# A gMLP / Mamba-2 / SwiGLU layer on one core: gating matmuls in halves, inverse roots one iteration later, running sums fetched earlier, and some stores issued by ScalarE

## The chip, the cores and the metric

The kernel runs as one program on one core of a Trainium2 chip. A core has five instruction streams that run by themselves and meet at semaphores: TensorE (PE in the profile; PEld is its weight load), VectorE (DVE), ScalarE (ACT), GpSimd (POOL) and SyncE (SP). SP computes nothing here; it issues the transfers between HBM and the on-chip memory, and before the change it issues every one of them. An engine works through its instructions in order, so an instruction that waits holds up all behind it on the same engine, a transfer that waits on SP included. The metric is device microseconds (us) from launch to end; a run's number is that of the core.

## The reference, cut to what matters

One layer on 2048 latent tokens of width 1024, with 256 context tokens that only feed the scan's first states:

```python
hl = _rms(x) * norm1_w * (1 + sc1) + sh1               # adaLN
proj = hl @ w_in                                       # u, v | z, x, B, C, dt
# group A: gated MLP, 8 heads of 128, chunks of 128 tokens
u, v = split(gelu(proj[..., :2048]), 2)
v = _rms(v per head) * gm_norm_w
mixed = einsum('hts,bcshd->bcthd', gm_ws, v) + gm_bs
gm_out = u * mixed
# group B: Mamba-2 scan forward and backward, 16 heads of 64, chunks of 128 tokens
xbc = silu(centred_conv(x, B, C))
y = ssd_forward(xbc, dt_f) + flip(ssd_backward(flip(xbc), flip(dt_b))) + xs * D
ssd_out = _rms(y * silu(z), per half of 512) * ssd_norm_w
x = x + g1 * (concat(gm_out, ssd_out) @ w_out)
x = x + g2 * swiglu(_rms(x) * norm2_w * (1 + sc2) + sh2)
out = _rms(x) * final_norm_w
```

In the scan a chunk's decay between two tokens is exp of a difference of running sums (`a_cs`) along the chunk.

## The kernel before

Every large product is in float32, split into a high and a low part: `mm3` (L224) runs three 128x512 matmuls for each of 8 pieces of the inner dimension, 24 for one output tile of 128x512, into one of three PSUM banks called `mmp`. Five more banks, `smp`, serve all else. Tokens are worked in two blocks of 1024. On-chip buffers of 128x520 floats come from a pool of 14, `tma`, which loads, temporaries and results waiting for their store all share. Results that later stages need go through HBM: `rec` (the convolved x, B, C by chunk), `fscr` (running sums), `zscr`, `mscr` (mixing), `gmscr`, `sscr` (scan output), `r3scr` (its inverse roots), `x2scr` (residual).

The stages in order: adaLN and the context (to about 100 us of the profiled span); `xbc` of block 1 (to about 281); **run 1**, with `proj_v`, `proj_u`, `proj_z` of block 1 as main work and the context states, the backward scan of chunks 15 to 8, input statistics and adaLN weights beside it (to 573); `xbc` of block 0 (to 765); **run 2** (765 to 1560); then the SwiGLU layer.

In run 2 the main work is `proj_z`, `proj_v`, `proj_u` of block 0 and four times `out_half` (the output product), 16 or 17 steps each, 113 in all; a step is one `mm3` with what follows it. Beside it `ssd_bwd` and `ssd_y` run as a generator that is advanced 2.61 steps for each step of main work (`SIDE`), which sets the order in which instructions are put on every engine.

`ssd_y` has 32 iterations, one for each chunk `c` and half `g`. In iteration i it loads the records of i+2, runs `y_seg` of i+1 (the decay matrices, in two quarters `q`: two running-sum rows spread over 128 partitions come in, ScalarE adds a bias at L757, VectorE subtracts and takes the minimum at L758, ScalarE exponentiates, GpSimd multiplies at L762), then `y_out` of i (TensorE products, sums, the product with `zscr` at L798, the square sums at L799), then `y_store` of i-1 (four transposes L806, a copy L808, a store L809). `y_seg` begins with the load of the backward state at L745. After every eighth iteration `y_rstd` works out the inverse roots of 512 tokens: 12 small VectorE instructions (L815 and `newton`, L242 to L247), a transpose on TensorE (L819), a copy (L821) and a store (L822).

`proj_v` collects four chunks `c` of `v`, normalises them, and then, while the next four are computed, runs `mixing` on them after the `mm3` of c = 2: for each of 4 heads it loads the head's 128x128 weights and its bias row (L627, L628) into one of two buffers `gw`, runs 4 matmuls (L631) and one VectorE instruction (L633). The last four chunks are mixed at the end, after the last step.

A store passed to `behind` is issued by `flush` (L584) after the next `mm3`.

Of the kernel before, what the change touches and what calls it, by code (L numbers as in the profile page):

```python
# [14 lines left out]
P = 128  # L15
# [6 lines left out]
TB = 512  # L22
# [61 lines left out]
def kernel(ctx: ExitStack, tc: tile.TileContext, xT, ctxp, cc, crow, wad1, wad2, vecs, rows,  # L84
# [244 lines left out]
    for k in range(KT):  # L329
        t = xin()  # L330
# [132 lines left out]
    def to_tok(o, n, q, ch):  # L463
        g, coff = (ch // 4, R_X + (ch % 4) * P) if ch < 8 else (ch - 8, R_B)
        nt = n // P
        ps = smp()
        for c in range(nt):
            PE.transpose(out=ps[:, c * P:(c + 1) * P], in_=o[:, c * P:(c + 1) * P], identity=ident)
        t = tma()
        S.copy(t[:, :n], ps[:, :n])  # L470
        DMA.dma_start(rec[q][g][:, :, coff:coff + P].rearrange("c p x -> p c x"),
                      t[:, :n].rearrange("p (c x) -> p c x", x=P))

    def xbc(blk, hs, hc, tail):
# [120 lines left out]
    def stat_terms(hs, c, us, off):  # L595
# [6 lines left out]
            r.append((hs[j][k][:, 0, cs], hs[j][k][:, 1, cs], hi[:, fs], lo[:, fs]))  # L602
        return r

    def proj_u(blk, hs):
        for h0 in range(0, 8, 2):
            us = [unit(U_U + h0), unit(U_U + h0 + 1)]
            for j in range(2):
                ts_ = slice((blk * 2 + j) * TB, (blk * 2 + j + 1) * TB)
                for i, (hi, lo) in enumerate(us):  # L610
                    m = tmp()
                    DMA.dma_start(m[:, :TB], mscr[h0 + i][:, ts_])
                    ps = mmp()
                    mm3(ps, [(hi[:, k * P:(k + 1) * P], lo[:, k * P:(k + 1) * P], hs[j][k][:, 0, :], hs[j][k][:, 1, :]) for k in range(KT)])
                    flush()
                    t = gelu2(ps, tmp)
                    V.tensor_tensor(out=t[:, :TB], in0=t[:, :TB], in1=m[:, :TB], op=ALU.mult)
                    behind(gmscr[h0 + i][:, ts_], t[:, :TB])
                    yield

    def proj_v(blk, hs):
        def mixing(hh, j, vh):
            ts_ = slice((blk * 2 + j) * TB, (blk * 2 + j + 1) * TB)
            for h in range(4):
                hd = hh * 4 + h
                gw = sp.tile([P, 2, P], F32, name="gw", tag="gw", bufs=2)
                DMA.dma_start(gw[:, 0, :], gmw[:, hd * P:(hd + 1) * P])  # L627
                DMA.dma_start(gw[:, 1, :], gmb[:, hd * P:(hd + 1) * P].broadcast_to([P, P]))  # L628
                ps = smp()
                for c in range(4):  # L630
                    PE.matmul(ps[:, c * P:(c + 1) * P], lhsT=vh[c][:, h * P:(h + 1) * P], rhs=gw[:, 0, :], start=True, stop=True)  # L631
                m = tmp()
                V.scalar_tensor_tensor(out=m[:, :TB].rearrange("p (c x) -> p c x", x=P), in0=ps.rearrange("p (c x) -> p c x", x=P),  # L633
                                       scalar=vec[:, V_GN + hd:V_GN + hd + 1], in1=gw[:, 1:2, :].broadcast_to([P, 4, P]),
                                       op0=ALU.mult, op1=ALU.add)
                behind(mscr[hd][:, ts_], m[:, :TB])

        prev = None
        for hh in range(2):
            us = [unit(U_V + hh * 4 + i) for i in range(4)]  # L640
            for j in range(2):
                vh = []
                ms = sml()[:, :16]
                for c in range(4):
                    ps = mmp()
                    mm3(ps, stat_terms(hs, j * 4 + c, us, 0))
                    flush()
                    v = gelu2(ps, xin)
                    sq = tmp()
                    for h in range(4):  # L650
                        S.activation(sq[:, h * P:(h + 1) * P], v[:, h * P:(h + 1) * P], AF.Square, accum_out=ms[:, c * 4 + h:c * 4 + h + 1])
                    vh.append(v)
                    if c == 2 and prev is not None:
                        mixing(*prev)
                    if c < 3:
                        yield
                V.tensor_scalar(out=ms, in0=ms, scalar1=1.0 / P, scalar2=4 * EPS, op0=ALU.mult, op1=ALU.add)
                r = newton(ms, 16)
                for c, v in enumerate(vh):
                    V.tensor_tensor(out=v[:, :TB].rearrange("p (a b) -> p a b", b=P), in0=v[:, :TB].rearrange("p (a b) -> p a b", b=P),  # L660
                                    in1=bc(r[:, c * 4:c * 4 + 4].rearrange("p (a o) -> p a o", o=1), P), op=ALU.mult)
                yield
                prev = (hh, j, vh)
        mixing(*prev)
        yield

    zdone = [0]
# [67 lines left out]

    hbp = []

    def y_load(pools, i, c, g):
        return {"rc": load_rec(pools[i % 3 == 2], c, g, True)}

    def y_seg(st, c, g):
        rc = st["rc"]
        Gt = []
        hb = hbp[0].tile([P, TB], F32, name="hb", tag="hb") if g else tma()[:, :TB]
        DMA.dma_start(hb, hscr[c][:, g * TB:(g + 1) * TB])  # L745
        st["hb"] = hb
        for q in range(2):
            h0 = g * 8 + q * 4
            fb, bb = tma()[:, :TB], tma()[:, :TB]
            o = ((c % 4) * 32 + h0) * P  # L750
            DMA.dma_start(fb, fscr[c // 4][:, o:o + TB].broadcast_to([P, TB]))
            DMA.dma_start(bb, fscr[c // 4][:, o + 16 * P:o + 16 * P + TB].broadcast_to([P, TB]))
            A = tma()[:, :TB]
            for e in range(4):
                es = slice(e * P, (e + 1) * P)
                h = h0 + e
                S.activation(bb[:, es], bb[:, es], AF.Identity, bias=nacs[:, c, h:h + 1])  # L757
                V.scalar_tensor_tensor(out=fb[:, es], in0=fb[:, es], scalar=acs[:, c, h:h + 1], in1=bb[:, es], op0=ALU.subtract, op1=ALU.min)  # L758
                S.activation(A[:, es], rc[:, R_WF:R_WF + P], AF.Copy, scale=dt_sb[:, c, h:h + 1])
                V.scalar_tensor_tensor(out=A[:, es], in0=rc[:, R_WB:R_WB + P], scalar=dt_sb[:, c, 16 + h:17 + h], in1=A[:, es], op0=ALU.mult, op1=ALU.add)  # L760
            S.activation(fb, fb, AF.Exp)
            G.tensor_tensor(out=A, in0=A, in1=fb, op=ALU.mult)  # L762
            Gt.append(A)
            yield
        st["G"] = Gt
        if c < NCH - 1:
            xd = tma()[:, :TB]
            G.tensor_tensor(out=h3(xd), in0=h3(rc[:, R_X:R_X + TB]), in1=hv(ddt[:, c, g * 8:g * 8 + 8]), op=ALU.mult)
            st["xd"] = xd
        yield  # L770
# [32 lines left out]
    def y_store(ya, c, g):  # L803
        ps = smp()
        for i in range(4):
            PE.transpose(out=ps[:, i * P:(i + 1) * P], in_=ya[:, i * P:(i + 1) * P], identity=ident)  # L806
        t = tma()[:, :TB]
        S.copy(t, ps)  # L808
        DMA.dma_start(sscr[c // 4][g * TB:(g + 1) * TB, (c % 4) * P:(c % 4 + 1) * P].rearrange("(i p) t -> p i t", p=P),  # L809
                      t.rearrange("p (i t) -> p i t", t=P))  # L810
        yield

    def y_rstd(tb, ms):

        V.tensor_scalar(out=ms, in0=ms, scalar1=1.0 / TB, scalar2=4 * EPS, op0=ALU.mult, op1=ALU.add)  # L815
        r = newton(ms, 8)
        yield
        ps = smp()
        PE.transpose(out=ps[0:8, :P], in_=r, identity=ident)  # L819
        t = tma()  # L820
        S.copy(t[0:8, :P], ps[0:8, :P])  # L821
        DMA.dma_start(r3scr[tb].rearrange("g (c x) -> (g c) x", x=P), t[0:8, :P])  # L822

    def ssd_y(rp):
        its = [(c, g) for c in range(NCH) for g in range(2)]
        st = {}
        st[0] = y_load(rp, 0, *its[0])
        yield from y_seg(st[0], *its[0])
        st[1] = y_load(rp, 1, *its[1])
        store = None  # L830
        for i, (c, g) in enumerate(its):
            if i + 2 < len(its):
                st[i + 2] = y_load(rp, i + 2, *its[i + 2])
            if i + 1 < len(its):
                yield from y_seg(st[i + 1], *its[i + 1])
            if g == 0 and c % 4 == 0:
                ms = sml()[:, :8]
            y = yield from y_out(st.pop(i), c, g, ms[:, g * 4 + c % 4:g * 4 + c % 4 + 1])
            if store is not None:
                yield from y_store(*store)  # L840
            store = (y, c, g)
            if g == 1 and c % 4 == 3:
                yield from y_rstd(c // 4, ms)
        yield from y_store(*store)

    def load_mix(tb, half):
        hj = []
# [572 lines left out]
```

## Time and profile before

| | |
|---|---|
| median of 3 runs | 2975.28 us (2970.3 to 2985.91) |
| profiled execution, its own time | 2980.2 us |
| its span, first to last instruction | 2978.4 us |
| TensorE busy in the span | 2815.9 us (95%) |
| VectorE busy | 1977.8 us (66%) |
| ScalarE busy | 1272.8 us (43%) |
| mean granted TensorE clock | 0.971 of full speed |
| transfers | 528.03 MB, 177 GB/s over the span |

The span is the profiled execution from its first to its last instruction; 1.8 us of its time lie outside it. Busy time of TensorE is a time in which some matmul was under way, at whatever clock was granted: a matmul of 512 columns takes twice as long at the lower of the two levels, and then counts twice. What is lost is therefore partly idle time and partly busy time at the lower clock. Where a table of stretches is shown, the first column is the stretch in us from the span's start; a column PEclk of 0.51 means that nearly the whole stretch ran at half of full speed (1.2 GHz of 2.4).

### The profile page before, as it was taken

What the parts mean: (1) busy time and instruction counts of PE and PEld (TensorE: products, weight loads), DVE (VectorE), ACT (ScalarE), POOL (GpSimd) and SP (SyncE); (2) the same over time, 40 slices, a digit from 0 to 9 for tenths busy, and PEclk for the clock granted to TensorE, in tenths of its full rate; (3) what the DMA queues carried; (4) which work ended last, traced back from release to release, by engine and by line L of the source; (5) the groups of instructions that cost most, each with busy time, mean ns of one, the idle gap of its engine ahead of it and who ended that gap; (6) DMA issues with size and microseconds to landing.
All of it is one profiled execution on the core that took longest, in us unless ns stands there. A gap on an engine that the chain in (4) does not pass through costs nothing. (4 is left out here: it accounts for less than half of the span.)

```text
span 2978.4 us, 36719 instructions
## 1 busy us (share of the span) xinstructions
PE 2815.9 (95%) x12478; PEld 2252.8 (76%) x12478; DVE 1977.8 (66%) x3012; ACT 1272.8 (43%) x2360; POOL 637.6 (21%) x550
## 2 busy tenths in 40 slices
PE   7999989999998898998979899999999899999997
PEld 2788778788677676776768688888778788888885
DVE  6776866886678788777876655556766544445555
ACT  4445343344356455443543533333544333333443
POOL 3100000101132232322302344444210322221000
PEclk8999999999999999998989899999999999999998
DMA  6222567742755588786758444445766333334664
GB/s 223 91 88 89 178 217 236 247 135 85 229 178 147 173 248 250 221 257 214 245 164 278 165 152 163 159 151 181 253 218 204 127 106 106 106 100 132 227 192 155
DMA packets 296744, 528.03 MB, mean 177 GB/s; under 512 B 28998, under 2 KB 89830, under 8 KB 296556
## 3 DMA queue, kind: packets, MB, share of 16 engines
q1 hardware_dynamic: 296556, 525.69, 55.3%
q8 instruction: 98, 1.61, 0.2%
q14 instruction: 90, 0.74, 0.1%
HBM read 382.94 MB, written 142.64 MB: 176 GB/s over the span
## 5 line engine op out<-in xcount | busy, mean ns | idle before, releaser
L1028 DVE TENSOR_TENSOR hl<-w,hl 128x1024 fp32r<-128x1024 f32 x286 | 373.5, 1312 | 317.0 <-ACT hl L1027 133.4
L1027 ACT CAST hl<-w 128x1024 fp32r<-128x1024 f32 x286 | 299.0, 1049 | 442.6 <-PE smp L1273 167.8
L234 PE MATMUL mmp<-actt,whi 128*128 128x512 f32 x1120 | 456.1, 407 | 24.9 <-DVE tma L592 15.4
L236 PE MATMUL mmp<-actt,wlo 128*128 128x512 f32 x1120 | 444.3, 397 | 0.0
L235 PE MATMUL mmp<-actt,whi 128*128 128x512 f32 x1120 | 443.1, 396 | 0.2 <-DVE actt L861 0.2
L1144 PE MATMUL mmp<-hl,hl 128*128 128x512 f32 x704 | 277.4, 394 | 9.3 <-DVE hl L1028 9.3
L1142 PE MATMUL mmp<-hl,hl 128*128 128x512 f32 x704 | 277.9, 395 | 7.8 <-ACT t L1167 3.5
L1143 PE MATMUL mmp<-hl,hl 128*128 128x512 f32 x704 | 277.4, 394 | 0.0
L234 PEld LDWEIGHTS mmp<-actt,whi 128*128 128x128 f32 x1120 | 214.6, 192 | 74.9 <-DVE tma L592 17.6
L235 PEld LDWEIGHTS mmp<-actt,whi 128*128 128x128 f32 x1120 | 214.8, 192 | 47.3 <-issue 4.3
L236 PEld LDWEIGHTS mmp<-actt,wlo 128*128 128x128 f32 x1120 | 214.1, 191 | 46.2 <-issue 0.5
L234 PE MATMUL mmp<-whi,actt 128*128 128x512 f32 x512 | 211.1, 412 | 2.4 <-DVE tma L679 2.4
L1142 PE MATMUL smp<-hl,hl 128*128 128x512 f32 x528 | 208.6, 395 | 0.0
L1143 PE MATMUL smp<-hl,hl 128*128 128x512 f32 x528 | 207.3, 393 | 0.0
L235 PE MATMUL mmp<-wlo,actt 128*128 128x512 f32 x512 | 206.8, 404 | 0.0
L236 PE MATMUL mmp<-whi,actt 128*128 128x512 f32 x512 | 206.8, 404 | 0.0
L1144 PE MATMUL smp<-hl,hl 128*128 128x512 f32 x528 | 206.7, 392 | 0.0
L1034 DVE TENSOR_TENSOR t<-smp,t 128x512 f32<-128x512 f32 x88 | 60.4, 687 | 181.6 <-PE smp L1144 132.5
L1034 POOL TENSOR_TENSOR w<-w 128x512 f32<-128x512 f32 x44 | 59.0, 1341 | 486.9 <-DVE hl L1028 320.9
L1144 PEld LDWEIGHTS mmp<-hl,hl 128*128 128x128 f32 x704 | 133.7, 190 | 38.9 <-DVE hl L1028 10.2
L1142 PEld LDWEIGHTS mmp<-hl,hl 128*128 128x128 f32 x704 | 133.5, 190 | 38.4 <-ACT t L1167 4.2
L456 DVE SCALAR_TENSOR_TENSOR tma<-xin,cw,tma 128x512 f32<-128x512 f32 x192 | 144.2, 751 | 21.9 <-ACT tma L454 16.3
(275 smaller groups left out, 5755.5 us busy)
## 6 DMA issues: line engine op xcount, KB each, us to landing
w<-in_wall_dram SPq DMA_DIRECT2D x110, 512.0 KB, 4.0
ws<-in_wall_dram SPq DMA_DIRECT2D x104, 512.0 KB, 3.8
ascr<-t SPq DMA_DIRECT2D x154, 256.0 KB, 3.8
w<-ascr SPq DMA_DIRECT2D x154, 256.0 KB, 3.7
tma<-fscr SPq DMA_DIRECT2D x128, 256.0 KB, 6.2
w<-wscr SPq DMA_DIRECT2D x88, 256.0 KB, 3.1
t<-x2scr SPq DMA_DIRECT2D x76, 256.0 KB, 4.3
w<-in_wall_dram SPq DMA_DIRECT2D x66, 256.0 KB, 3.0
```

Of the source, the lines that this page charges most:

```text
L234: PE.matmul(ps, lhsT=lh, rhs=rh, start=(i == 0), stop=False)
L235: PE.matmul(ps, lhsT=lh, rhs=rl, start=False, stop=False)
L236: PE.matmul(ps, lhsT=ll, rhs=rh, start=False, stop=(i == n - 1))
L456: V.scalar_tensor_tensor(out=acc[:, :n], in0=raw[:, j:j + n], scalar=cw[:, ch, j:j + 1], in1=acc[:, :n], op0=ALU.mult, op1=ALU.add)
L1027: S.copy(hi, x)
L1028: eng.tensor_tensor(out=lo, in0=x, in1=hi.bitcast(F32), op=ALU.subtract)
L1034: eng.tensor_tensor(out=o, in0=a, in1=b, op=ALU.add)
L1142: PE.matmul(ps, lhsT=hi[:, ms_], rhs=t[:, 0, :], start=first and k == 0, stop=False, skip_group_check=not first)
L1143: PE.matmul(ps, lhsT=hi[:, ms_], rhs=t[:, 1, :], start=False, stop=False, skip_group_check=not first)
L1144: PE.matmul(ps, lhsT=lo[:, ms_], rhs=t[:, 0, :], start=False, stop=k == 3, skip_group_check=not first)
```

## The change

Five edits:

1. `proj_v`: the loads of the weights are taken out of `mixing` into `gate_load`, which is called one step before the matmuls that need them; `mixing` does two heads at a time, after the `mm3` of c = 2 and of c = 3. The last four chunks of a `proj_v` are mixed in `proj_u`, after its second and third `mm3` (`tails`).
2. `ssd_y`: the transpose, copy and store of the inverse roots become a function `rows`, which is called one iteration later, after that iteration's `y_store` (for the last, after the last `y_store`).
3. `y_seg`: the loads of the running sums become `f_load`. Those of the first quarter of i+2 are issued at the end of `y_out` of i, those of the second quarter at the start of the first.
4. `y_store` and `rows`: ScalarE, which has just made the copy, issues the store itself (36 transfers).
5. `to_tok`, called by `xbc`: the same for the 50 stores of the convolved records.

```diff
@@ to_tok
-        DMA.dma_start(rec[q][g][:, :, coff:coff + P].rearrange("c p x -> p c x"),
+        S.dma_start(rec[q][g][:, :, coff:coff + P].rearrange("c p x -> p c x"),
                       t[:, :n].rearrange("p (c x) -> p c x", x=P))
@@ proj_u
+    tails = []
...
                     flush()
+                    if tails and (j or i):
+                        tails.pop(0)()
                     t = gelu2(ps, tmp)
@@ proj_v
-        def mixing(hh, j, vh):
-            ts_ = slice((blk * 2 + j) * TB, (blk * 2 + j + 1) * TB)
-            for h in range(4):
+        gws = []
+
+        def gate_load(hh, h0):
+            for h in range(h0, h0 + 2):
                 hd = hh * 4 + h
                 gw = sp.tile([P, 2, P], F32, name="gw", tag="gw", bufs=2)
                 DMA.dma_start(gw[:, 0, :], gmw[:, hd * P:(hd + 1) * P])
                 DMA.dma_start(gw[:, 1, :], gmb[:, hd * P:(hd + 1) * P].broadcast_to([P, P]))
+                gws.append(gw)
+
+        def mixing(hh, j, vh, h0):
+            ts_ = slice((blk * 2 + j) * TB, (blk * 2 + j + 1) * TB)
+            for h in range(h0, h0 + 2):
+                hd = hh * 4 + h
+                gw = gws.pop(0)
                 ps = smp()
...
-                    if c == 2 and prev is not None:
-                        mixing(*prev)
+                    if prev is not None:
+                        if c == 1:
+                            gate_load(prev[0], 0)
+                        if c >= 2:
+                            mixing(*prev, 2 * c - 4)
+                        if c == 2:
+                            gate_load(prev[0], 2)
...
-        mixing(*prev)
+        gate_load(prev[0], 0)
+        tails.append(lambda: (mixing(*prev, 0), gate_load(prev[0], 2)))
+        tails.append(lambda: mixing(*prev, 2))
         yield
@@ y_seg
+    def f_load(c, g, q):
+        fb, bb = tma()[:, :TB], tma()[:, :TB]
+        o = ((c % 4) * 32 + g * 8 + q * 4) * P
+        DMA.dma_start(fb, fscr[c // 4][:, o:o + TB].broadcast_to([P, TB]))
+        DMA.dma_start(bb, fscr[c // 4][:, o + 16 * P:o + 16 * P + TB].broadcast_to([P, TB]))
+        return fb, bb
...
         for q in range(2):
             h0 = g * 8 + q * 4
-            fb, bb = tma()[:, :TB], tma()[:, :TB]
-            o = ((c % 4) * 32 + h0) * P
-            DMA.dma_start(fb, fscr[c // 4][:, o:o + TB].broadcast_to([P, TB]))
-            DMA.dma_start(bb, fscr[c // 4][:, o + 16 * P:o + 16 * P + TB].broadcast_to([P, TB]))
+            fb, bb = st["f"].pop(0)
+            if q == 0:
+                st["f"].append(f_load(c, g, 1))
@@ y_store
-        DMA.dma_start(sscr[c // 4][g * TB:(g + 1) * TB, (c % 4) * P:(c % 4 + 1) * P].rearrange("(i p) t -> p i t", p=P),
+        S.dma_start(sscr[c // 4][g * TB:(g + 1) * TB, (c % 4) * P:(c % 4 + 1) * P].rearrange("(i p) t -> p i t", p=P),
                       t.rearrange("p (i t) -> p i t", t=P))
@@ y_rstd
         r = newton(ms, 8)
-        yield
-        ps = smp()
-        PE.transpose(out=ps[0:8, :P], in_=r, identity=ident)
-        t = tma()
-        S.copy(t[0:8, :P], ps[0:8, :P])
-        DMA.dma_start(r3scr[tb].rearrange("g (c x) -> (g c) x", x=P), t[0:8, :P])
+
+        def rows():
+            ps = smp()
+            PE.transpose(out=ps[0:8, :P], in_=r, identity=ident)
+            t = tma()
+            S.copy(t[0:8, :P], ps[0:8, :P])
+            S.dma_start(r3scr[tb].rearrange("g (c x) -> (g c) x", x=P), t[0:8, :P])
+
+        return rows
@@ ssd_y
             y = yield from y_out(st.pop(i), c, g, ms[:, g * 4 + c % 4:g * 4 + c % 4 + 1])
+            if i + 2 < len(its):
+                st[i + 2]["f"] = [f_load(*its[i + 2], 0)]
             if store is not None:
                 yield from y_store(*store)
+                if rows is not None:
+                    rows()
+                    rows = None
             store = (y, c, g)
             if g == 1 and c % 4 == 3:
-                yield from y_rstd(c // 4, ms)
+                rows = y_rstd(c // 4, ms)
+                yield
         yield from y_store(*store)
+        rows()
```

## Rows read from the trace of the kernel before

**Rows 1.** The page, part 1: engine, busy us, share of the span, instructions.
```profile
PE 2815.9 (95%) x12478; PEld 2252.8 (76%) x12478; DVE 1977.8 (66%) x3012; ACT 1272.8 (43%) x2360; POOL 637.6 (21%) x550
```

**Rows 2.** Busy time by stage: xbc of block 1, run 1, run 2.
```profile
core 0: us, PE busy (x) PEld busy (x) DVE busy (x) ACT busy (x) POOL busy (x), PEclk, DMA share, GB/s
100.00:281.00 181.00, 180.74 (x984) 155.65 (x983) 133.80 (x196) 86.06 (x159) 10.60 (x57) 1.00 0.31 92
281.00:573.00 292.00, 279.04 (x1222) 219.66 (x1220) 209.94 (x384) 109.65 (x263) 8.13 (x6) 0.99 0.64 210
...
765.00:1560.00 795.00, 723.54 (x3230) 563.43 (x3229) 614.84 (x1199) 390.07 (x1014) 198.61 (x156) 0.95 0.70 213
```

**Rows 3.** TensorE's waits in run 1: us in total, times, longest.
```profile
PE mmp L234 <- DVE tma L592: 6.3, 2, 3.2
PE smp L631 <- issue: 2.2, 1, 2.2
```

**Rows 4.** TensorE's waits in run 2, the same columns.
```profile
PE smp L819 <- DVE sml L247: 22.9, 4, 8.3
PE smp L631 <- DMA gw<-in_gmw_dram: 13.2, 6, 6.2
PE mmp L234 <- DVE tma L592: 9.2, 2, 8.0
...
PE smp L779 <- POOL tma L762: 4.1, 2, 2.9
PE smp L776 <- DVE tma L782: 2.8, 1, 2.8
...
PE smp L777 <- DVE tma L783: 1.4, 1, 1.4
```

**Rows 5.** Busy time while TensorE waits at L819: first of four stretches, their sum.
```profile
985.80:991.00 5.20, 0.00 (x0) 0.00 (x0) 5.13 (x19) 2.10 (x7) 1.04 (x1) 0.79 0.34 102
...
sum 22.60, PE 0.01 PEld 0.00 DVE 19.00 ACT 6.68 POOL 3.04; mean PE 0.00 PEld 0.00 DVE 4.75 ACT 1.67 POOL 0.76
```

**Rows 6.** TensorE at the lower clock around the four waits at L819.
```profile
core 0: us, PE busy (x), PEclk, DMA share, GB/s
988.70:995.50 6.80, 4.43 (x11) 0.51 0.24 73
...
sum 30.70, PE 19.96; mean PE 4.99
```

**Rows 7.** The same around waits at L631: second of three stretches, their sum.
```profile
927.20:934.00 6.80, 3.83 (x13) 0.51 0.66 197
...
sum 17.00, PE 12.37; mean PE 4.12
```

**Rows 8.** The same around three waits behind the running sums: the third, the sum.
```profile
1323.20:1333.40 10.20, 9.77 (x29) 0.51 0.63 198
sum 23.80, PE 18.73; mean PE 6.24
```

**Rows 9.** Busy time while TensorE waits longest at L631, columns of rows 2.
```profile
924.00:930.10 6.10, 0.00 (x0) 0.00 (x0) 6.10 (x9) 4.86 (x13) 1.27 (x1) 0.78 0.20 59
```

**Rows 10.** VectorE's waits in run 2: us in total, times, longest.
```profile
DVE tma L758 <- ACT tma L757: 74.0, 39, 5.7
DVE tma L895 <- PE mmp L236: 16.8, 4, 6.0
```

**Rows 11.** ScalarE's waits in run 2, the same columns.
```profile
ACT tma L757 <- DMA tma<-fscr: 117.9, 44, 6.8
```

**Rows 12.** The waits of SP's queue in run 2, the same columns.
```profile
SPq L745 <- DVE tma L793: 38.9, 13, 14.6
SPq L809 <- ACT tma L808: 31.3, 19, 4.6
...
SPq L809 <- ACT tma L759: 16.6, 9, 3.9
```

**Rows 13.** The second running-sum load of a quarter (L752).
```profile
DMA to landing us min/median/max: 4.6/6.9/7.9
```

**Rows 14.** The store of the scan output on SP (L809), ns min/median/max.
```profile
L809 SPq DMA_DIRECT2D sscr<-tma x32: 370/371/463, 844.6 to 1524.6; - x32
```

More of the change, by code (lines that the diff above doesn't have):

```diff
@@ L827, in ssd_y @@
         st[0] = y_load(rp, 0, *its[0])
+        st[0]["f"] = [f_load(*its[0], 0)]
         yield from y_seg(st[0], *its[0])
         st[1] = y_load(rp, 1, *its[1])
-        store = None
+        st[1]["f"] = [f_load(*its[1], 0)]
+        store = rows = None
         for i, (c, g) in enumerate(its):
```

## The prediction

> **What bounds the kernel now.** I read the page first: TensorE is busy 95% of the span, VectorE 66% [rows 1]. So TensorE sets the time, and an edit pays only where TensorE stands idle or runs at its lower clock. The stretches by stage say where that is. In `xbc` of block 1 it is busy 180.74 of 181 us, in run 1 279.04 of 292, in run 2 723.54 of 795 with a mean granted clock of 0.95 [rows 2]. Run 2 alone has 71.5 us of idle time, and all five edits but the `xbc` stores act there or in run 1.
>
> Third come TensorE's waits, and they name the edits' targets: in run 2, 22.9 us at L819 for the end of `newton`, in four waits of up to 8.3 us, and 13.2 us at L631 for the gating weights; in run 1, 2.2 us more at L631, put down to no releaser [rows 3, 4]. Then four waits on results of `y_seg` or of VectorE work queued beside it: L779 4.1 us, L776 2.8, L777 1.4, and of L234's 9.2 us the longest, 8.0 [rows 4].
>
> Last I asked for TensorE's busy time where the granted clock is half, around these waits. A wait is dear twice: the clock falls to its lower level (1.2 GHz of 2.4) near its end, after the idle time, and the matmuls that follow take double time. 19.96 us of matmuls ran so around the L819 waits, 12.37 around L631, 18.73 around the three places of the running sums [rows 6 to 8]. At full clock each needs half, so half of each sum is lost time.
>
> **The roots (edit 2).** Removed: 22.9 us idle [rows 4] and 19.96/2 = 10.0 us at the lower clock [rows 6], 32.9 in all. The transpose itself stays, and its inputs are ready an iteration later. Would TensorE find VectorE just as late at the next bank? In the four stretches VectorE is busy 19.00 of 22.6 us; only in the first is it busy throughout, 5.13 of 5.20 [rows 5]. In the `out_half` steps, where the other three lie, VectorE then waits for TensorE: L895 waits 16.8 us in four waits of up to 6.0 [rows 10]. So I keep the three in full and half of the first, (5.2 + 4.43/2)/2 = 3.7 less: **-29**. Bounds: -33, and -16 if VectorE takes half back everywhere. Behind the root's copy on ScalarE stand the next activations, which no longer wait for it; and the roots' HBM rows come an iteration later, long before their readers except for the last eight iterations, where the reader follows a few steps on.
>
> **The gating weights (edit 1).** Removed: 13.2 + 2.2 us idle [rows 3, 4] and 12.37/2 = 6.2 at the lower clock [rows 7]: 21.6. The weights of a half are now asked for one step ahead. A step of run 2 lasts 795/113 = 7.0 us, so a load that lands within 6.9 us, the median of one four times as large [rows 13], is in before its matmuls. SP still waits for L633 before the second `gate_load`, with `y_seg`'s loads behind it, but that order existed before. In the longest wait VectorE is busy 6.10 of 6.10 us [rows 9], so TensorE would soon want a bank that VectorE has not emptied: there I keep half, (6.2 + 3.83/2)/2 = 4.0 less: **-18**. Bounds: -22 and -9. L592's 6.3 us in run 1 [rows 3] I leave at nothing, with -6.3 as its far end.
>
> **The running sums (edit 3).** ScalarE waits at L757 for these loads 44 times, 117.9 us in all, 2.7 each [rows 11]; VectorE waits for ScalarE in turn, 74.0 us [rows 10]. TensorE pays 4.1 + 2.8 + 1.4 + 8.0 = 16.3 us idle [rows 4] and 18.73/2 = 9.4 at the lower clock [rows 8]: 25.7. How early are the loads now? A quarter is one generator step, 7.0/2.61 = 2.7 us, and both quarters are asked for one step sooner. The first also moves ahead of SP's waits at L745 (38.9 us in 13) and of the store it used to follow, L809, 31.3 + 16.6 us [rows 12], which leaves SP altogether. A lead of 2.7 us against a mean wait of 2.7 takes away the ordinary waits and shortens the long ones, up to 6.8. I take half: **-13**. Bounds: -26 and 0.
>
> **ScalarE's stores (edits 4, 5).** Each costs SP 0.37 us [rows 14]; I price one on ScalarE alike, since no row shows one there. 36 x 0.37 = 13 us come onto ScalarE in run 2, where it is busy 390 of 795 us [rows 2]. What is queued behind such a store, activations that VectorE and so TensorE's banks wait for, is late by that much. Some three in ten of it should reach TensorE: **+4**, bounds 0 and +13. A store also holds ScalarE until its own copy is finished; that I leave in the upper bound. The 50 stores of `xbc` I cost at nothing: in block 1's stage ScalarE is busy 86.06 of 181 us and TensorE loses 0.26 us [rows 2]; if that cover went, they would be 50 x 0.37 = 18 us of ScalarE's time.
>
> The Trainium skill speaks against the edit: "DMA: Bandwidth & Descriptors", section "Issuing engines are not separate DMA queues", says that issuing from several engines saves only the sequencer's issue time. By that rule the stores give back 32 x 0.37 = 12 us of SP's time and nothing else. The trace differs in one respect: what SP loses at L809 is 47.9 us of waiting for ScalarE, four times the issue time [rows 12, 14].
>
> **New waits.** With 56 us out, VectorE's 614.84 busy us [rows 2] stand against 739 instead of 795: 83% instead of 77%. It is not the bound, but its queue bunches, above all where `load_mix` and `y_out` meet. I charge **+7**, bounds 0 and +20.
>
> **Sum.** -29 - 18 - 13 + 4 + 7 = -49 us. The profiled execution took 2980.2 us for a span of 2978.4, and gives 2931; it lies 4.9 us over the median of the runs shown, 2975.3, from which I count: **2926**. All gains in full and no costs: 2975.3 - 33 - 22 - 26 - 6 = 2888.
>
> **The rivals.**
>
> *VectorE takes over* (18%). TensorE's waits move from L819 and L631 to L234, for banks that VectorE empties late. For: VectorE is busy in most of every wait [rows 5, 9]. Against: L895's waits for TensorE [rows 10]. Half of the roots and weights, a quarter of the sums: -16 - 9 - 6 + 4 + 7 = -20, 2955.
>
> *The fetch is not ahead* (15%). The change does not do what it says: SP, freed of L809, stands at the next wait instead, L745 or the record load, and the running sums go out as late as now; a lead of 2.7 us is also less than even the shortest landing of 4.6 us [rows 13]. Edit 3 gives nothing: -29 - 18 + 4 + 7 = -36, 2939. This is what the Trainium skill's rule on issuing engines would make of edit 4.
>
> *All is given back* (12%). The idle time shown is slack of a fixed order in which VectorE's and ScalarE's chain through `y_seg` and `y_out` sets the pace; TensorE merely waits elsewhere. For: ScalarE and VectorE wait for each other more than TensorE waits for either [rows 10, 11]. Against: those waits are themselves for the loads that come earlier. 2975, within 10.
>
> *SP stands for buffers: slower* (10%). Running-sum tiles are taken from the 14 `tma` buffers sooner; at the first quarter of `y_seg` four are held instead of two. If no buffer is free, SP stands at `f_load`, with records, weights and `zscr` behind it. Price: of ScalarE's 117.9 us at L757, 25.7 reached TensorE, 0.22. For 62 early pairs that wait w us each, 62 x 0.22 x w = 13.6 w. Without edit 3's gain the rest is -36, so it decides from w = 2.6 us; at 3.7 the kernel is 0.5% slower, at 5 it takes 2975.3 - 36 + 68 = 3007. For: SP's waits at L745 are for buffers freed by VectorE, 3.0 us on average, up to 14.6 [rows 12]. Against: halves of `mixing` hold two results at once instead of four.
>
> **How the numbers follow.** Half a per cent, 15 us, is about what a measurement of this kernel can tell from no change. The forecast gets 45%; its own range, with its terms' bounds taken half together, is 2905 to 2950. All of the first three cases, and a little of the fourth, are faster by over 0.5%: 77%. Within: most of the fourth and some of the last, 13%. Slower: 10%. The range must hold 8 in 10: below 2890 nearly all gains would have to come in full (about 4%); above, the buffers' case and some of the giving back, 16% or so, are left out from 2971 on. Range 2890 to 2971.
>
> **What the profile after would show.** Right: no wait at L819's successor; none at L631 for `gw` above 1 us; ScalarE's wait for `fscr` at half or less of 117.9 us; run 2 near 795 - 47 = 748 us with a clock of 0.98. Each term can fail alone: a large wait of L234 for L592 or L895 means that VectorE took over; `fscr` waits still near 118, that the fetch is not ahead; new waits of SP at `f_load`, that buffers ran out. Most of all the prediction is wrong if run 2 keeps its length while TensorE's waits change their names.

## The result, and the profile after

The changed kernel takes 2952.0 us (median of 5 runs, 2946.9 to 2953.2), the kernel before 2974.1 beside it (5 runs). The ratio is 0.9918, 95% interval 0.9896 to 0.9941, which is 24 us of 2974 (the medians are 22 us apart). The forecast was 2926, with 2890 to 2971 as its range: the sign and the range hold, and about half of the gain is missing. The profiled executions differ by more, 2978.4 against 2950.2 us of span, because that of before was a long one, 6 us over the median; below, stages are read from the profiles and prices from the ratios.

The page, parts 1 and 3, of the kernel after (part 1: busy us, share, instructions; part 3: packets, MB, share of 16 engines):

```profile
PE 2811.6 (95%) x12478; PEld 2250.1 (76%) x12478; DVE 1967.1 (67%) x3012; ACT 1274.2 (43%) x2360; POOL 642.0 (22%) x550
...
q1 hardware_dynamic: 255756, 505.48, 52.7%
q10 hardware_dynamic: 40800, 20.21, 2.4%
```

Against [rows 1] the busy times have hardly moved; what changed is idle time. The second queue, q10, is not in the page of before: it carries what ScalarE issues. The stages, run 1 and run 2 of after:

```profile
core 0: us, PE busy (x) PEld busy (x) DVE busy (x) ACT busy (x) POOL busy (x), PEclk, DMA share, GB/s
...
281.00:562.00 281.00, 276.23 (x1225) 218.79 (x1223) 209.19 (x386) 111.87 (x266) 8.96 (x6) 0.99 0.66 218
...
755.00:1528.50 773.50, 721.43 (x3235) 562.64 (x3234) 611.24 (x1199) 389.65 (x1014) 198.92 (x156) 0.96 0.71 219
```

Run 1 went from 292 to 281 us, run 2 from 795 to 773.5 [rows 2]; the prediction had 748 us and a clock of 0.98 for run 2. In run 2 TensorE's idle time fell from 71.5 to 52.1 us, but its busy time only from 723.5 to 721.4, and the granted clock only from 0.95 to 0.96. So what came back is idle time; of the time at the lower clock, half of which each term counted as a gain, nearly all stayed. TensorE's waits in run 2 of after (us in total, times, longest):

```profile
PE mmp L234 <- DVE tma L932: 10.0, 2, 8.7
PE smp L643 <- DMA gw<-in_gmw_dram: 8.2, 4, 2.9
PE smp L802 <- DVE tma L807: 7.0, 1, 7.0
PE smp L831 <- DVE tma L823: 5.3, 1, 5.3
PE smp L845 <- DVE tma L807: 3.9, 1, 3.9
...
PE smp L845 <- DVE sml L247: 0.7, 1, 0.7
```

L845 is the root's transpose, L819 before; its 22.9 us [rows 4] are 4.6. L643, the gating matmul (L631 before), still waits 8.2 us for weights asked for a step ahead. L932 is before's L895, the instruction that empties `out_half`'s banks. Of the rest, L802 in `y_out` is before's L777, where 1.4 [rows 4] and 2.0 us stood; the transposes of `y_store` (L831) are a new place. In run 1 the waits at L592 and L631 [rows 3] are gone altogether. ScalarE's and VectorE's waits in run 2 of after, the same columns:

```profile
ACT tma L782 <- DMA tma<-fscr: 84.7, 38, 5.8
```
```profile
DVE tma L783 <- ACT tma L782: 58.5, 37, 4.0
DVE tma L823 <- DMA tma<-zscr: 20.9, 8, 4.9
```

L782 and L783 are before's L757 and L758: 117.9 us became 84.7 [rows 11], 74.0 became 58.5 [rows 10].

### The profile page after: what moved, and what is told of

Its sections match the earlier page's. It is cut to its first block, busy times and chain, and to the rows that moved or that the text cites. A ratio compares the mean times of both kernels' runs of the same rounds, so it can differ in the third digit from the quotient of the medians.

```text
span 2950.2 us, 36694 instructions
## 1 busy us (share of the span) xinstructions
PE 2811.6 (95%) x12478; PEld 2250.1 (76%) x12478; DVE 1967.1 (67%) x3012; ACT 1274.2 (43%) x2360; POOL 642.0 (22%) x550
## 5 line engine op out<-in xcount | busy, mean ns | idle before, releaser
L1071 POOL TENSOR_TENSOR w<-w 128x512 f32<-128x512 f32 x44 | 67.5, 1535 | 480.2 <-DVE hl L1065 313.5
L787 POOL TENSOR_TENSOR tma<-tma 128x512 f32<-128x512 f32 x64 | 92.6, 1447 | 341.2 <-ACT tma L786 144.4
L1179 PEld LDWEIGHTS mmp<-hl,hl 128*128 128x128 f32 x704 | 133.3, 189 | 41.4 <-ACT t L1204 8.0
```

Of the source, the lines that this page charges most:

```text
L1071: eng.tensor_tensor(out=o, in0=a, in1=b, op=ALU.add)
L1179: PE.matmul(ps, lhsT=hi[:, ms_], rhs=t[:, 0, :], start=first and k == 0, stop=False, skip_group_check=not first)
```

## The experiments

Medians and ratios are against runs of the kernel before beside them on the same chip; "us" is the ratio's distance from 1 times 2974.

**The four parts alone.** Each takes only its own hunks of the diff into the kernel before. e1_roots, with the rows' store left on SP:

```diff
-        yield
-        ps = smp()
-        PE.transpose(out=ps[0:8, :P], in_=r, identity=ident)
...
+        def rows():
+            ps = smp()
...
+        return rows
```

> The kernel before with edit 2 alone (the roots' transpose, copy and store one iteration later, the store still on SP). Theory A, the terms of the prediction hold and add up: -29 us, near 2945, no wait of TensorE for newton above 1 us, run 2 shorter by 29 us. Theory B, what one wait gives back is mostly lost at the next because SP's queue stands at its waits for VectorE all the same: TensorE's wait for newton goes, but new waits for VectorE results replace half of it, -10 to -16 us, near 2961. Theory C, VectorE is the pace maker: within 5 us of before.

Measured: 2972.3, ratio 0.9991 (0.9980 to 1.0002), -3 us and not told apart from nothing, as Theory C has it by time. TensorE's waits in run 2 of e1_roots (L903 is before's L895, L820 the transpose):

```profile
PE mmp L234 <- DVE tma L903: 20.1, 3, 10.8
PE smp L631 <- DMA gw<-in_gmw_dram: 15.4, 5, 6.5
PE mmp L234 <- DVE tma L592: 9.4, 3, 6.8
PE smp L779 <- POOL tma L762: 7.6, 4, 2.8
...
PE smp L820 <- DVE tma L782: 2.0, 1, 2.0
```

The transpose all but stopped waiting: 3.1 us are left of 22.9. But `out_half`'s banks, which L903 empties, are now late by 20.1 us in three waits, where the same pair in run 2 of before shows one:

```profile
PE mmp L234 <- DVE tma L895: 8.7, 1, 8.7
```

That one, at run 2's last step, is there in e1_roots too (8.72 us), so the wait of 10.8 us is the new one. The waits at L631 and L779 grew by 2.2 and 3.5 us. VectorE's timeline of e1_roots, from within the longest wait to its end, says why it is there (start, us):

```profile
1395.37 1.88 DVE L869 TENSOR_TENSOR actt<-xin,actt 128x512 fp32r<-128x512 f32 x3
1397.18 2.07 DVE L866 SCALAR_TENSOR_TENSOR xin<-xin,vec,tma 128x512 f32<-128x512 f32 x3
1399.16 0.68 DVE L869 TENSOR_TENSOR actt<-xin,actt 128x512 fp32r<-128x512 f32 x1
1399.77 3.39 DVE L866 SCALAR_TENSOR_TENSOR xin<-xin,vec,tma 128x512 f32<-128x512 f32 x5
1403.08 0.74 DVE L903 SCALAR_TENSOR_TENSOR tma<-mmp,m_sb,tma 128x512 f32<-128x512 f32 x1
```

L866 and L869 are `load_mix` for the next half: work of VectorE without a gap, in front of the one instruction that frees TensorE's bank. Before, TensorE waited 5.6 us behind the same burst, at L787 (to 1411.6 us), after it had lost 8.3 us at the transpose, a wait that ended at 1351.8. So of this one root 5.2 us are seen to move to the burst. For the other three no such place was found: over all of run 2, idle time in these two profiles falls by some 11 us, of which the long execution of before can explain a part. The repeated times leave 3 us of the gain; where the rest went is not shown.

e2_gates, `proj_v` and `proj_u` with `gate_load`, halves and tails:

```diff
-        def mixing(hh, j, vh):
+        def mixing(hh, j, vh, h0):
...
+                gw = gws.pop(0)
...
+                        if c == 1:
+                            gate_load(prev[0], 0)
```

> The kernel before with edit 1 alone (mixing in halves, gating weights one step ahead, the last four chunks mixed in the next projection). Theory A: -18 us, near 2956, with run 1 shorter by 3 us only. Theory B: the gain in run 2 is at most 10 us, but run 1, where the end of proj_v stops blocking SP's input loads, gains some 10 us too, since the changed kernel gained 11 us there: near 2955 to 2960. The two differ in where: run 1 by -3 (A) or by -10 (B).

Measured: 2948.2, 0.9915 (0.9899 to 0.9931), -25 us. Its stages, run 1 and most of run 2, which begins at about 750 us here:

```profile
281.00:560.00 279.00, 274.76 (x1226) 217.89 (x1224) 208.97 (x387) 109.16 (x262) 10.45 (x6) 1.00 0.67 221
755.00:1530.00 775.00, 717.38 (x3209) 560.82 (x3209) 605.62 (x1194) 390.17 (x1013) 203.25 (x156) 0.95 0.69 217
```

Run 1 is 13 us shorter than before's 292, of which 4.3 are busy time, at a clock of 1.00 instead of 0.99; run 2, from 750 to 1530, is 15 us shorter than 795. That is nearer to Theory B by its place. In run 1 ScalarE's longest wait for the input's loads fell; before, the gating loads of four heads stood in front of them on SP, now those of two do. ScalarE's wait in run 1, before and then in e2_gates:

```profile
ACT tma L261 <- DMA tma<-in_xT_dram: 23.7, 10, 11.4
```
```profile
ACT tma L261 <- DMA tma<-in_xT_dram: 18.5, 13, 2.9
```

In the kernel before, the 11.4 us end at 413.2 us; L592 and, through it, TensorE were late just behind (417.1). That wait of 3.20 us is one of the two that make up L592's 6.3 [rows 3]. Between 380 and 418 us SP stood 7.3 us at the gating loads (L627), for buffers that L633 frees; in e2_gates it stands 2.5 us there.

e3_fetch, `f_load` and its calls in `y_seg` and `ssd_y`:

```diff
-            fb, bb = tma()[:, :TB], tma()[:, :TB]
...
+            fb, bb = st["f"].pop(0)
+            if q == 0:
+                st["f"].append(f_load(c, g, 1))
```

> The kernel before with edit 3 alone (running sums asked for one generator step sooner; all stores still on SP). Theory A: -13 us, near 2961, ScalarE's wait for the running sums at half of 117.9 us. Theory B: SP stands at the store of the scan output and at its other waits before it reaches the early loads, ScalarE's wait stays over 90 us, and the time is within 8 us of before.

Measured: 2956.3, 0.9939 (0.9923 to 0.9955), -18 us. Neither theory holds whole: the time is A's and better, but ScalarE's wait for the running sums stays at 114.0 us, as B has it. In run 2 TensorE's wait for the gating weights, which this edit does not touch, falls from 13.2 [rows 4] to 6.1 us.

e4_stores, the three stores alone (one of them shown):

```diff
-        DMA.dma_start(sscr[c // 4][g * TB:(g + 1) * TB, ...
+        S.dma_start(sscr[c // 4][g * TB:(g + 1) * TB, ...
```

> The kernel before with edits 4 and 5 alone (ScalarE issues its 36 stores of run 2 and the 50 of xbc). Theory A: +4 us, near 2978, SP's waits in run 2 fall by the 58 us at these stores. Theory B: SP's waits in run 2 keep their sum near 524 us, moved to flush and to the loads that need a buffer, and the time is within 5 us of before.

Measured: 2977.8, 1.0013 (1.0002 to 1.0024), +4 us. SP's waits in run 2 do not fall: they sum to 544 us against 525, which is Theory B. The four alone sum to -42; together they give -24. So some of the parts stand in each other's way.

**Which parts?** e8_gatefetch is before with edits 1 and 3; e9_allsp adds edit 2, so it is the changed kernel with all 86 stores back on SP; e7_noxbc is the changed kernel with only `xbc`'s 50 back on SP:

```diff
# e9_allsp against the changed kernel, in to_tok, y_store and rows
-        S.dma_start(
+        DMA.dma_start(
```

> The kernel before with edits 1 and 3 (gating weights ahead, running sums ahead), roots and all stores as before. Theory A, parts add: -25 - 18 = -43 us, near 2931. Theory L, run 2 has a second limit some 25 us below its time before (VectorE's queue around the loads of the output product's inputs), which either edit reaches alone: 2944 to 2952.

> The changed kernel with all 86 stores back on SP (edits 1, 2 and 3). Theory A, parts add: -25 - 18 - 2 = -45 us, near 2929. Theory L: 2944 to 2952, as without the roots. If ScalarE's stores are what spoils the changed kernel, it is some 8 us or more faster than it, 2944 or less; if they are neutral, 2950.

> The changed kernel without edit 5: the 50 stores of the convolved records back on SP. Theory S, these stores cost TensorE time in xbc because ScalarE also empties its banks there (alone, edits 4 and 5 made run 2 start some 6 us later): 4 to 7 us faster than the changed kernel, near 2947, with run 2 starting 5 us sooner. Theory N, their cost is nothing, as the prediction had it: within 2 us of the changed kernel, 2952.

Measured: e8_gatefetch 2943.4, 0.9902 (0.9886 to 0.9919), -29. e9_allsp 2935.0, 0.9880 (0.9863 to 0.9898), -36. e7_noxbc 2945.3, 0.9906 (0.9891 to 0.9922), -28. Edits 1 and 3 together lose 14 us of their sum, and e8_gatefetch lies at the edge of Theory L; but e9_allsp at 2935 lies between both theories, so there is no one limit at 2944. A part of the 14 can be named: the wait for gating weights is 13.2 us before, 9.9 in e2_gates, 6.1 in e3_fetch and 6.0 in e8_gatefetch, so both edits draw on the same wait. The roots on top of edits 1 and 3 bring about 7 us (the intervals overlap). The stores take back 12 of the 36 (15 to 17 by the medians): some 8 by run 2's 36, some 4 by the 50 of `xbc`, each of the two steps by itself within its intervals.

How do they take it back? First the issue and landing of the scan output's store in after:

```profile
L834 ACTq DMA_DIRECT2D sscr<-tma x32: 366/367/425, 832.9 to 1492.3; - x32
...
DMA to landing us min/median/max: 3.0/5.4/8.7
```

then the same store's landing in e9_allsp, where SP issues it:

```profile
DMA to landing us min/median/max: 2.5/3.6/4.7
```

The issue costs ScalarE what it cost SP, 0.37 us [rows 14], so the estimate there was right. But the transfer lands later, 5.4 us against 3.0 in before and 3.6 in e9_allsp, and until then it holds a `tma` buffer out of 14. SP's queue takes those buffers for its loads, and stands for a store that has not landed; its waits of that kind in run 2 of after, all but one of 0.5 us:

```profile
SPq L614 <- DMA sscr<-tma: 10.1, 2, 5.9
...
SPq L915 <- DMA sscr<-tma: 6.4, 2, 5.8
...
SPq L761 <- DMA sscr<-tma: 3.2, 1, 3.2
...
SPq L633 <- DMA sscr<-tma: 2.3, 1, 2.3
...
SPq L760 <- DMA sscr<-tma: 2.0, 1, 2.0
...
SPq L632 <- DMA sscr<-tma: 1.9, 1, 1.9
```

That is 25.9 us at the loads of `proj_u`, `out_half`, the running sums (L760, L761) and the gating weights (L632, L633). e9_allsp has 9.0 us of them and before 2.2. But e4_stores has 25.2 us of them as well and is only 4 us slower than before: the sum of these waits is not the price.

**Is it the buffers?** e5_after16 is the changed kernel with 16 `tma` buffers, e12_noxbc16 the same of e7_noxbc, e10_allsp16 of e9_allsp and e6_before16 of before. The room comes from narrower tiles and two small constants in another pool:

```diff
-NTMA = 14
+NTMA = 16
...
-        return tpa.tile([P, 520], F32, name="tma", tag="tma")
+        return tpa.tile([P, TB], F32, name="tma", tag="tma")
...
-        return sp.tile([P, 64], F32, name="sml", tag="sml")
+        return sp.tile([P, 16], F32, name="sml", tag="sml")
```

> The changed kernel with 16 buffers in the shared pool instead of 14 (room from narrower small tiles). Theory of the rival on buffers, SP stands for a free buffer at the early loads and with it the gain: 10 us or more faster than the changed kernel, SP's waits in run 2 well under 534 us and ScalarE's wait for the running sums under 60 us. If buffers are not what is short: within 4 us of 2952.

> As the run with all stores on SP and 16 buffers, but with the 36 stores of run 2 on ScalarE. If ScalarE's stores cost through the buffers they hold (the scan output lands in 5.0 to 5.4 us from ScalarE, in 3.0 to 4.4 from SP), 16 buffers hide it: within 3 us of the run with all stores on SP. If they cost ScalarE's own time: 8 to 10 us slower than that run, as with 14 buffers.

> Edits 1, 2 and 3 with all stores on SP, and 16 buffers in the shared pool. If the two losses found so far, ScalarE's stores (-17 us when put back) and the short pool (-17 us when widened), are separate: 2952 - 17 - 17 = 2918. If both are the same shortage of buffers (ScalarE's stores land later and hold their buffers longer): 2930 to 2936, as with either alone.

> The kernel before with 16 buffers in the shared pool, nothing else. If the pool is short only because the change holds buffers longer: within 4 us of before, 2973. If the pool was short before as well: 2955 to 2960, the 17 us that the changed kernel gains by it.

| | 14 buffers | 16 buffers |
|---|---|---|
| edits 1 to 3, stores on SP | 0.9880 (0.9863 to 0.9898) | 0.9865 (0.9848 to 0.9882) |
| with run 2's 36 on ScalarE | 0.9906 (0.9891 to 0.9922) | 0.9862 (0.9845 to 0.9879) |
| with all 86 on ScalarE | 0.9918 (0.9896 to 0.9941) | 0.9872 (0.9855 to 0.9888) |
| before | 1 | 1.0029 (1.0016 to 1.0041) |

With 16 buffers the three versions are alike, 2935.0, 2934.1 and 2934.9 us. Wherever ScalarE issues stores the two buffers bring 13 to 14 us, with intervals apart; where SP does, 4 or nothing, with intervals that overlap; and the kernel before they make 9 us slower, for which I have no cause. So the price of run 2's stores goes with the small pool: shown, for the pool together with the narrower tiles that made room for it; the narrower tiles with 14 buffers were not run. That it is the wait at one particular load is not shown. Nor is the share of `xbc`'s stores: in e5_after16, with 16 buffers, the first gating matmul still comes at 318.0 us, against 314.5 in e12_noxbc16, one profile each. With 16 buffers SP still waits for stores of this kind, in e12_noxbc16 37.5 us in run 2, most of it here:

```profile
SPq L915 <- DMA sscr<-tma: 17.1, 5, 6.4
SPq L584 <- DMA sscr<-tma: 8.1, 3, 4.1
SPq L822 <- DMA sscr<-tma: 6.9, 1, 6.9
```

So longer waits of this kind than in after cost nothing here. These are `out_half`'s fetch, the flush of queued stores and `zscr`'s load. At the running sums and `proj_u`'s load there are none any more; that these were the dear ones is only argued. Of the signs named for e5_after16 the time came true (14 us faster), and SP's waits in run 2 fell from 538 to 517 us, but ScalarE's wait for the running sums stayed at 82.9.

**Is `zscr` the next limit?** VectorE's wait for it had grown from 8.0 us before to 20.9. e11_zahead is e10_allsp16 with that load at the start of `y_out`:

```diff
     def y_out(st, c, g, ms):
+        zt = tma()[:, :TB]
+        DMA.dma_start(zt, zscr[c][:, g * TB:(g + 1) * TB])
```

> The run with all stores on SP and 16 buffers, and the load of zscr asked for at the start of y_out, two generator steps sooner. VectorE waits 18 to 21 us for this load in the versions with the changed order (8 before): if that is the next limit, 5 to 8 us faster than without it; if VectorE's own queue is, no difference.

Measured: 2938.1, 0.9885 (0.9871 to 0.9900), against 0.9865 without it. No gain: the wait was slack, or the buffer held longer costs as much, so `zscr` is not the next limit.

## Why the prediction was half right

**What bounds the kernel.** Right: the gain lies in runs 1 and 2 (11 and 21.5 us in the profiles) and is TensorE's idle time. Wrong was to add half of the time at the lower clock to each term. Run 2 of e9_allsp, with all stores on SP, reads:

```profile
752.00:1516.00 764.00, 719.37 (x3226) 560.40 (x3225) 607.46 (x1198) 389.62 (x1013) 203.08 (x156) 0.96 0.72 221
```

Its idle time is 44.6 us, 27 less than before, its busy time 4 less. The waits that remain lower the clock as the old ones did: in after the nine matmuls behind the wait of 8.7 us ran at a granted clock of 0.52 (1524.35 to 1528.2 us), those from 1528.2 to 1531 at 1.00. It is not a rule that this time never comes back: in run 2 of e5_after16 the idle time is 45 us as well, but the busy time 711 and the clock 0.98.

**The roots, -29.** This is the step that failed. The wait went, as the term said, but the kernel gained 3 us by it alone and about 7 beside edits 1 and 3, where the term had 29; that is as much as the 25 us by which the forecast missed. The prediction kept three of four stretches in full because VectorE waited for TensorE in those steps [rows 10]. That average hid `load_mix`'s bursts, where VectorE is late. For one root e1_roots shows the wait at the transpose taken in place of a longer wait at the next burst, 10.8 us instead of 5.6; for the others the place is open. This is the rival "VectorE takes over", for this term alone, and it took more than the half that was priced. That the rival's time, 2955, lies near the measured one is luck: its weights and sums gave 15 us, the measured ones 25 and 18.

**The gating weights, -18.** Mis-sized: -25 alone. About half of it is in run 1 (13 us, run 2 15), where L592's 6.3 us [rows 3] were left at nothing although the end of `mixing` and the input's loads share SP's queue. In run 2 the weights are still late by 8.2 us in after, 2.3 in e9_allsp, where the prediction allowed no wait above 1 us. SP asks for them a step ahead in program order, but stands at buffers on the way: in after the weights that are late at 917.07 us were issued at 914.67, behind waits of SP of 16.2 us at the load of the backward state (L771) and of 10.4 at a record load (L730), both for buffers; those late at 952.01 had stood 3.9 us at the load itself, for one of the two `gw`.

**The running sums, -13.** Right in size: -18, interval -13 to -23, but not by the way that the term gives. The lead was to take away ScalarE's ordinary waits, and the mark was a wait for `fscr` of half or less of 117.9 us. In e9_allsp, faster than after, it stands at

```profile
ACT tma L782 <- DMA tma<-fscr: 114.4, 43, 8.1
```

Wherever SP issues the scan's stores it is 110 us or more, without edit 3 (110.7 in e1_roots, 111.3 in e2_gates) and with it (114.0 in e3_fetch, 110.3 in e8_gatefetch); wherever ScalarE does, it is shorter (96.4 in e4_stores, 82.7 to 84.7 in the others), and none of those is faster for it. So it was the move of the stores that shortened this wait, and its total says little of what TensorE pays: the 0.22 us per us by which the rival on buffers was priced has no support. Of the rival "the fetch is not ahead" the sign is there and the price, no gain, is not. Some 7 us of e3_fetch's gain stand at the gating weights, which the term did not count; why this edit brings them sooner the runs do not show. So the size is in part luck.

**ScalarE's stores, +4 and nothing for `xbc`.** Right alone (+4 for all 86), wrong in place: +12 beside the other edits. The term priced the issue and left out the buffer that a store holds until it lands. Buffers were in the prediction, as the rival "SP stands for buffers", but laid to the early loads; e9_allsp has the early loads, stands 9.0 us for stores and gains 4 us or nothing by a larger pool, while after has the late stores as well. In `xbc` the prediction counted on ScalarE's idle time as cover. The profile of e4_stores shows the first gating matmul at 320.0 us against 315.1 in before, with TensorE's idle time from 100 us to there at 0.6 us in both: if these stores cost time, it is not seen as a wait.

The Trainium skill, "DMA: Bandwidth & Descriptors", section "Issuing engines are not separate DMA queues", says that issuing from several engines saves only the time that the issuing engine takes to start a transfer. The runs agree that there was nothing more to win: e4_stores gained nothing, and with 16 buffers e10_allsp16 and e12_noxbc16 are equal to within 1 us.

**New waits, +7.** The parts alone give -3 - 25 - 18 = -46, edits 1 to 3 together -36: +10, near enough. The whole, measured: -3 - 25 - 18 + 10 + 12 = -24.

By terms, the 25 us that are missing are 26 of the roots, 8 of the stores and 3 of the new waits, less 7 of the weights and 5 of the sums.

Open remain why before is slower with 16 buffers, and at which load the pool of 14 costs TensorE its time. Two more buffers, with the narrower tiles, moved the kernel before by 9 us, so a price of that size may hang on the order of the instructions around it. The fastest versions, e12_noxbc16, e5_after16, e10_allsp16 and e9_allsp, lie within 1 us of each other by median, at 2934 to 2935 us (measured on different chips), 17 under the changed kernel by median and 12 to 17 by ratio; of these e9_allsp needs no more buffers, only its stores back on SP.

## What to carry to other kernels

A wait that is removed may pay only up to the next burst of the engine behind it: look along TensorE's next steps for a stretch of that engine without gaps before counting it in full, and do not count the lower clock in full while other waits remain. The total of a wait on an engine that is not the bottleneck is no price: here ScalarE's went from 114 to 85 us while the kernel became slower. A store that is moved to another engine has two prices, its issue and the buffer that it holds until it lands; here, where a pool of 14 is shared with loads, the second was the larger. Price parts in the changed order, not in the old one: the stores cost 4 us alone and 12 among the other edits.

## What was not expected of the hardware

The same 256 KB store, issued in the same 0.37 us, landed later when ScalarE issued it into a queue of its own than when SP did, in every pair that differs in this alone or in this and `xbc`'s stores: 5.7 against 3.0 us in the median (e4_stores, before), 5.4 and 5.0 against 3.6 (after, e7_noxbc, e9_allsp), 4.4 and 4.6 against 3.7 (e5_after16, e12_noxbc16, e10_allsp16). It is not the issuing engine alone: from SP it took 4.4 us in e8_gatefetch. The runs do not show why. Two more buffers of the same pool, with nothing else but tile widths and two constants changed, slowed the kernel before by 0.29% (0.16 to 0.41).
